# Attention of an encoder in whole f32 instead of split halves, and row sums from blocks added beforehand

## The chip, the cores and the metric

The kernel runs on one core of a Trainium2 chip. Its time is the device time of one execution in microseconds (us); lower is better. Before the change three runs had a median of 2032.31 us (2031.08 to 2033.2). A profiled execution of the same program, from which every duration below is read, took 2032.38 us, of which the trace covers a span of 2030.4 us.

The engines are named as in the profile: PE is the matrix engine (PEld its weight loads), DVE the vector engine, ACT the scalar engine, POOL the GpSimd engine, SP the queue that issues most transfers. PSUM is the memory in which PE leaves its products, in eight banks.

## The reference, cut to what matters

Two layers over 1024 tokens of width 1024, all in float32. One layer:

```python
h = _rmsnorm(x, g_pre_mix[l])
zf, zq, zk, zv, zm = jnp.split(h @ w_in[l], splits, axis=-1)
y_f = _fourier_mix(zf, w_fourier[l])                  # 256 wide
y_a = _window_attn(rope(zq), rope(zk), zv, sink[l])   # 8 query heads, 2 key heads, window of 128 either way
y_m = _memory_attn(zm, km, vm)                        # 4 heads over 256 memory rows
y = concat([_rmsnorm(y_f, gg[:256]), _rmsnorm(y_a, gg[256:768]), _rmsnorm(y_m, gg[768:])]) @ w_out[l]
x = x + _rmsnorm(y, g_post_mix[l])
gate, up = jnp.split(_rmsnorm(x, g_pre_ffn[l]) @ w_ffn_in[l], 2, axis=-1)
x = x + _rmsnorm((jax.nn.silu(gate) * up) @ w_ffn_out[l], g_post_ffn[l])
```

Heads are 64 wide. The three group norms before `w_out` each need the sum of squares of a token's row in their group.

## The kernel before, in words

Large products use a split: an f32 value is rounded to the shorter type `fp32r` (the high part, made on ACT) and the remainder (the low part, made on DVE or POOL) is rounded as well; three products of parts (`Acc.add`, L185) stand for one f32 product. A product of plain f32 operands is also possible; PE does it in two passes, so that the trace has two instructions for each.

A layer goes through these stages. The first layer's times are in brackets, the second layer's lie about 1005 us later.

- Fourier part, keys, values and memory queries (`kvz`, L714, and `kvz_turn`, L731; 60 to 126 us). `kvz_turn` transposes the memory queries on PE and `q_stacks` (L431) puts them into stacks: of two heads that lie on partitions 0 to 63 and 64 to 127, one stack has head 0's high part on the lower 64 partitions and its low part on the upper 64, and the other has head 1's, mirrored. `dup_stacks` (L420) writes a key's high part on both halves, and its low part on both halves. One product over 128 partitions then sums high and low parts of the query against the high part of the key, a second against the low part.
- Queries and memory attention (`q`, L761; `q_turn`, L766; `mem_scores`, L891; `mem_turn`, L917; `mem_values`, L928; 126 to 205 us). A call of `mem_scores` takes one head and 512 tokens: 8 fp32r products 256 wide.
- Attention of key head 0 (`att_units(0)`), woven with the Fourier and memory part of the output product (`fm_units`, L1006; 205 to 292 us). For each block of 128 queries, `att_scores` (L777) makes the scores of four query heads over up to 384 keys, two products a head (L788), DVE adds the mask and takes the maximum, ACT takes the exponential, POOL scales; `att_values` (L817) transposes the weights on PE (L825), splits them (L837) and multiplies (L840); `fold` adds the two halves.
- Attention of key head 1 (`att_units(1)`), woven with the rest of the output product (`out`, L1061), both norms and the transposes for the feed-forward part (`Blocks.tile`, L1099; 292 to 386 us). Here `att_values` takes plain f32 weights and values (L833): the product for the heads of even index writes PSUM partitions 0 to 63, that for the odd ones 64 to 127.
- Feed-forward (L1181, L1330).

`group_scale` (L980) makes the factor of a group norm: ACT squares the group's blocks (2 blocks of 128x128 for the memory group, 4 for the attention group), PE multiplies each block with a 128x2 tile of ones into the same PSUM tile (L988), DVE and POOL make the factor. It runs 16 times per layer.

PSUM tiles come from four pools, `sc`, `pT`, `av` and `pd`, of two tiles each; a tile has one bank. A tile's next user waits until its readers are done.

The order on each engine is set by a scheduler at build time: it places the instructions of all stages by readiness and priority, and each engine then works through its own list in that order. Rings such as `mps` and `yys` give out buffers in turn; a region in `TURNED` changes its type between f32 and fp32r.

## Time and profile before

| | |
|---|---|
| median of three runs | 2032.31 us |
| the profiled execution's own time | 2032.38 us |
| span in the trace | 2030.4 us |
| busy, share of the span | PE 98%, PEld 80%, DVE 74%, ACT 52%, POOL 34% |
| granted TensorE clock, mean | 0.994 of full speed |
| stages that the change touches | about 60 to 390 us and 1060 to 1395 us |

A busy time is the union of an engine's instructions in the trace. PE's ends are modelled and include the time in which a product drains, so the end of one matmul lies after the start of the next, and a short wait of PE can hide under such an end. Distances between starts are therefore used for the price of a matmul. A row of the timeline merges neighbouring instructions of a line: it has the start of the first, the time from there to the end of the last, and their count.

### The profile page before, as it was taken

To read this page: it belongs to the slowest core of one execution; us is meant where nothing else is said; L and a number is where in the kernel's file an instruction comes from. 1 tells how busy PE (TensorE), PEld (TensorE's weight loads), DVE (VectorE), ACT (ScalarE), POOL (GpSimd) and SP (SyncE) were. 2 spreads that over 40 slices of the span, in tenths; PEclk is the share of its full clock that TensorE was granted. 3 is DMA by queue.
4 is the path that set the end of the run, shared out by engine and by line. 5 is a ranking of instruction groups with operands and counts; after the bars stand their busy time and mean duration, and the time that the engine had idled before them with its cause. 6 is when DMAs were issued, how large, how long until landed. Compare 5 with 4: busy or idle time off the path is not lost.

```text
span 2030.4 us, 28325 instructions
## 1 busy us (share of the span) xinstructions
PE 1984.7 (98%) x9587; PEld 1631.2 (80%) x9587; DVE 1492.6 (74%) x2346; ACT 1049.7 (52%) x2204; POOL 684.9 (34%) x811
## 2 busy tenths in 40 slices
PE   8999999999999999999999999999999999999998
PEld 7877878778888888887888778877788888887886
DVE  5566767897877776778876668679786776778766
ACT  6476877643333333554555768686333333346441
POOL 4344445224334333002423644451433433410011
PEclk9999999999999999999999999999999999999999
DMA  6110333434333324879831113244333323269973
GB/s 213 62 58 22 109 104 115 146 109 130 104 109 100 103 88 139 297 266 324 286 142 54 54 58 115 85 144 135 106 118 114 116 82 114 96 209 354 314 265 125
DMA packets 181889, 288.56 MB, mean 142 GB/s; under 512 B 15560, under 2 KB 81648, under 8 KB 181744
## 3 DMA queue, kind: packets, MB, share of 16 engines
q1 hardware_dynamic: 173680, 267.88, 39.7%
q10 hardware_dynamic: 8064, 18.88, 2.4%
q8 instruction: 75, 1.23, 0.2%
q14 instruction: 70, 0.57, 0.1%
HBM read 220.11 MB, written 66.58 MB: 141 GB/s over the span
## 4 chain that ended last, share of the span: by engine, by line
PE 86%; DVE 5%; DMA 3%; ACT 2%; issue 2%; POOL 1%; SPq 0%; DVEq 0%; POOLq 0%; ACTq 0%
PE fo L1330 17%; PE qc L1181 11%; PE qx L1181 11%; PE qy L1181 11%; PE mo L187 8%; PE qz L1181 5%; PE kvp L187 4%; PE qp L187 3%; PE zT L187 2%; PE sc L788 2%; PE pT L825 2%; PE av L833 1%; PE qa L1181 1%; PE mav L932 1%; PE av L840 1%
## 5 line engine op out<-in xcount | busy, mean ns | idle before, releaser
L1330 PE MATMUL fo<-arena_r 128*128 128x512 f32 x1512 | 354.2, 391 | 6.0 <-ACT big L1355 3.8
L1330 PEld LDWEIGHTS fo<-arena_r 128*128 128x128 f32 x1512 | 283.6, 188 | 65.6 <-ACT big L1355 4.6
L176 ACT CAST arena_r<-arena_f 128x512 fp32r<-128x512 f32 (+2 forms) x344 | 185.9, 571 | 179.5 <-DMA arena_f<-actd 66.6
L1181 PE MATMUL qc<-arena_r,flex 128*128 128x512 f32 x912 | 220.2, 390 | 0.0
L177 DVE TENSOR_TENSOR arena_r<-arena_f,arena_r 128x512 fp32r<-128x512 f32 x262 | 182.0, 727 | 46.9 <-ACT arena_r L176 39.0
L1171 ACT CAST flex<-arena_f 128x512 fp32r<-128x512 f32 x148 | 91.9, 621 | 235.0 <-PE qy L1181 73.3
L1181 PEld LDWEIGHTS qc<-arena_r,flex 128*128 128x128 f32 x912 | 171.2, 188 | 37.0
L1181 PE MATMUL qy<-arena_r,flex 128*128 128x512 f32 x576 | 139.9, 390 | 2.3 <-ACT flex L1171 2.3
L1171 ACT CAST arena_r<-arena_f 128x512 fp32r<-128x512 f32 x92 | 57.1, 621 | 159.1 <-DVE arena_f L1168 63.6
L1172 DVE TENSOR_TENSOR flex<-arena_f,flex 128x512 fp32r<-128x512 f32 x148 | 110.9, 750 | 28.4 <-ACT flex L1171 28.2
L1181 PEld LDWEIGHTS qy<-arena_r,flex 128*128 128x128 f32 x576 | 107.9, 188 | 25.3 <-ACT flex L1171 2.7
L1215 POOL TENSOR_TENSOR arena_f<-arena_f 128x512 f32<-128x512 f32 x36 | 47.3, 1315 | 237.5 <-ACT arena_f L1186 237.5
L1181 PE MATMUL qx<-arena_r 128*128 128x512 f32 x360 | 119.5, 389 | 0.0
L1181 PE MATMUL qy<-arena_r 128*128 128x512 f32 x480 | 116.7, 390 | 0.0
L1172 DVE TENSOR_TENSOR arena_r<-arena_f,arena_r 128x512 fp32r<-128x512 f32 x92 | 68.2, 742 | 63.2 <-ACT arena_r L1171 62.8
L1181 PE MATMUL qz<-arena_r,flex 128*128 128x512 f32 x320 | 106.8, 395 | 0.0
L1181 PEld LDWEIGHTS qy<-arena_r 128*128 128x128 f32 x480 | 90.3, 188 | 18.9 <-ACT arena_r L1171 0.2
L1168 DVE TENSOR_TENSOR arena_f<-arena_f 128x512 f32<-128x512 f32 x90 | 98.1, 1098 | 5.5 <-DMA arena_f<-in_w_ffn_in 3.9
L1222 POOL TENSOR_TENSOR arena_f<-arena_f 128x512 f32<-128x512 f32 x36 | 60.0, 1667 | 120.2 <-DVE arena_f L1221 120.2
L187 PE MATMUL mo<-big,arena_r 128*128 128x512 f32 x384 | 100.2, 399 | 0.3 <-ACT arena_f L1031 0.2
L1181 PE MATMUL qx<-flex,flex 128*128 128x512 f32 x304 | 100.1, 390 | 0.0
L1242 POOL TENSOR_TENSOR arena_f<-arena_f,flex 128x512 f32<-128x512 f32 x32 | 51.8, 1619 | 139.5 <-ACT flex L1233 83.7
(315 smaller groups left out, 4659.8 us busy)
## 6 DMA issues: line engine op xcount, KB each, us to landing
arena_f<-in_w_ffn_out SPq DMA_DIRECT2D x264, 256.0 KB, 4.7
actd<-arena_f SPq DMA_DIRECT2D x154, 256.0 KB, 2.5
arena_f<-actd SPq DMA_DIRECT2D x154, 256.0 KB, 4.4
arena_f<-in_w_ffn_in SPq DMA_DIRECT2D x46, 512.0 KB, 3.7
big<-in_w_ffn_in SPq DMA_DIRECT2D x40, 512.0 KB, 4.5
arena_f<-in_w_in SPq DMA_DIRECT2D x40, 256.0 KB, 2.9
arena_f<-in_x SPq DMA_DIRECT2D x16, 512.0 KB, 4.3
arena_f<-in_w_out SPq DMA_DIRECT2D x32, 256.0 KB, 2.7
```

Source lines behind the costliest of these rows:

```text
L176: nc.scalar.copy(hi, src)
L177: return (lo_eng or nc.vector).tensor_tensor(out=lo, in0=src, in1=f32(hi), op=ALU.subtract)
L187: mm(self.dst, a, b, start=self.i == 0, stop=self.i == self.n - 1)
L788: mm(pt, lhs, self.kst[g][i][:, k0 * P : k1 * P], start=i == 0, stop=i == 1)
L1168: nc.vector.tensor_tensor(out=s, in0=x, in1=y, op=op)
L1171: self.cast = nc.scalar.copy(w[:, 0], s)
L1172: nc.vector.tensor_tensor(out=w[:, 1], in0=s, in1=f32(w[:, 0]), op=ALU.subtract)
L1181: mm(pt, a, b, start=start and n == 0, stop=n == 11, skip_group_check=not start)
L1215: G(out=self.u2, in0=self.u2, in1=self.p1, op=ALU.add)
L1222: G(out=self.p5, in0=self.p1, in1=self.p5, op=ALU.add)
L1242: (G if i % 2 else V).tensor_tensor(out=a[i], in0=c, in1=g[i], op=ALU.mult)
L1330: mm(pt, ab[:, 0, x, sl], ab[:, 1, y], start=new and first and j == 0, stop=last and j == 2, skip_group_check=not new)
```

## The change

It does four things.

- **Plain f32 in the window and memory attention.** `q_stacks`, `dup_stacks` and `fold` go. Queries, keys, values and memory queries are copied once, as f32. Two heads of 64 channels stay on partitions 0 to 63 and 64 to 127, and each score is one f32 product over its own 64 partitions: `att_scores` makes two such products, one for each half of the partitions, into the two banks of one tile. `mem_scores` takes two heads and 256 tokens per call instead of one head and 512. `att_values` uses for key head 0 what it had for key head 1; half of its copies for key head 0 go to DVE.
- **A new PSUM pool `s2`** with one tile of two banks for these scores. `qa` of the feed-forward part moves to it, `qc` goes from `pT` to `sc`, `qx` from `sc` to `pT`, `yfp` from `sc` to `av`.
- **Row sums.** `group_scale` adds the squared blocks on DVE (4 to 2 to 1, or 2 to 1) and makes one product with ones. Of 96 products with ones, 32 are left.
- **Storage.** More regions change their type in turn; blocks of the feed-forward part and the ring `yys` move.

```diff
-TURNED = {32: 8, 56: 8, 112: 8, 120: 4}
-PS_BUFS = {"sc": 2, "pT": 2, "av": 2, "pd": 2}
+PS_BUFS = {"sc": 2, "pT": 2, "av": 2, "pd": 2, "s2": 1}
...
-            raw = at(32, 2, NMEM)
-            nc.sync.dma_start(raw, kvd[self.l, :, 0:512].rearrange("p (i c) -> p i c", i=2))
+            self.k = at(32, 2, NMEM)
+            nc.sync.dma_start(self.k, kvd[self.l, :, 0:512].rearrange("p (i c) -> p i c", i=2))
             self.v = at(6, 2, 4, HD)
             nc.sync.dma_start(self.v, kvd[self.l, :, 512:1024].rearrange("p (t h d) -> p t h d", t=2, h=4))
-            km = shaped(reflex(F32R), (2, 2, 2, NMEM))
-            self.km = [km[:, i] for i in range(2)]
-            for ci in range(2):
-                dup_stacks([(self.km[ci][:, j, 0], self.km[ci][:, j, 1]) for j in range(2)], raw[:, ci])
 
...
+            self.kvr = {}
 
         def kvz(self, t):
             half, c = divmod(t, 4)
             if c == 0:
-                self.vst[half] = at(96 + 4 * half, 4, 2, 2, HD, dt=F32R)
-                z = at(104 + 8 * half, 2, 2, 512, dt=F32R)
-                self.zst[half] = [z[:, i] for i in range(2)]
                 if half == 0:
-                    kst = at(80, 2, 2, S, dt=F32R)
-                    self.kst = [[kst[:, i, j] for j in range(2)] for i in range(2)]
+                    self.v32 = turned(96, 2, 2, NT, HD)[:, 0]
+                    self.zf = turned(104, 2, 2, 512)
+                    self.kf = turned(80, 2, S)
             pt = ps([512], "kvp")
             wmov(self.wkvz, self.hT, t, pt)
             r = kvs(512)
             nc.scalar.activation(r, pt, AF.Copy, scale=rx[:, t : t + 1])
-            vst = self.vst[half][:, c]
-            split(vst[:, :, 0, :], vst[:, :, 1, :], r[:, P : 2 * P].rearrange("p (g d) -> p g d", g=2), nc.gpsimd)
+            nc.gpsimd.tensor_copy(self.v32[:, :, t, :], r[:, P : 2 * P].rearrange("p (g d) -> p g d", g=2))
...
-            q_stacks([self.zst[half][j][:, :, c * P : c * P + P] for j in range(2)], zt)
+            nc.scalar.copy(self.zf[:, half, :, c * P : c * P + P], zt)
...
                 ktf = self.kt.rearrange("p c t -> p (c t)")
                 sl = slice(half * 512, half * 512 + 512)
-                dup_stacks([(self.kst[g][0][:, sl], self.kst[g][1][:, sl]) for g in range(2)], ktf)
+                for g, copy in enumerate((nc.scalar.copy, nc.vector.tensor_copy)):
+                    for o in range(2):
+                        copy(self.kf[64 * o : 64 * o + 64, g, sl], ktf[64 * g : 64 * g + 64])
...
-                self.qst[half] = [at((64, 0)[half] + 8 * i, 4, 512, dt=F32R) for i in range(2)]
-            q_stacks([self.qst[half][j][:, :, c * P : c * P + P] for j in range(2)], qt)
+                self.qf[half] = turned((64, 72)[half], 4, 512)
+            nc.scalar.copy(self.qf[half][:, :, c * P : c * P + P], qt)
 
 
...
-            for h in range(4):
-                pt = ps([W], "sc", "sc")
-                lhs = self.qst[half][h % 2][:, 2 * g + h // 2, c * P : c * P + P]
-                for i in range(2):
-                    mm(pt, lhs, self.kst[g][i][:, k0 * P : k1 * P], start=i == 0, stop=i == 1)
-                nc.vector.tensor_tensor_reduce(
-                    out=es_[h // 2][:, h % 2, :W], in0=pt, in1=mask[:, m0 : m0 + W], op0=ALU.add, op1=ALU.max,
-                    scale=1.0, scalar=-3e38, accum_out=rmax[:, h : h + 1],
-                )
+            for hp in range(2):
+                pt = ps([2, 512], "sc", "s2")
+                pts = [pt[:, s, :W] for s in range(2)]
+                for s in range(2):
+                    r = slice(64 * s, 64 * s + 64)
+                    mm(pts[s], self.qf[half][r, 2 * g + hp, c * P : c * P + P], self.kf[r, g, k0 * P : k1 * P], start=True, stop=True)
+                for s in range(2):
+                    nc.vector.tensor_tensor_reduce(
+                        out=es_[hp][:, s, :W], in0=pts[s], in1=mask[:, m0 : m0 + W], op0=ALU.add, op1=ALU.max,
+                        scale=1.0, scalar=-3e38, accum_out=rmax[:, 2 * hp + s : 2 * hp + s + 1],
+                    )
             hs = slice(4 * g, 4 * g + 4)
...
-                if g:
-
-                    pf = self.pfs[self.pfi % 4]
-                    self.pfi += 1
-                    nc.scalar.copy(pf, pT.rearrange("p (k s) q -> p s k q", s=2))
-                    for s in range(2):
-                        rhs = pf[:, s].rearrange("p k q -> p (k q)")
-                        mm(av[64 * s : 64 * s + 64, 0 : 2 * P], self.v32[:, k0 + j], rhs, start=j == 0, stop=j == nk - 1)
-                    continue
-                pp = phs(2, 512, dt=F32R)
-                ph, pl = pp[:, 0], pp[:, 1]
-                split(ph, pl, pT.rearrange("p h q -> p (h q)"))
-                lhs = self.vst[(k0 + j) // 4][:, (k0 + j) % 4, g].rearrange("p a d -> p (a d)")
-                for i, p_ in enumerate((ph, pl)):
-                    mm(av, lhs, p_, start=j == 0 and i == 0, stop=j == nk - 1 and i == 1)
+                pf = self.pfs[self.pfi % 4]
+                self.pfi += 1
+                (nc.vector.tensor_copy if (self.pfi % 2 and not g) else nc.scalar.copy)(pf, pT.rearrange("p (k s) q -> p s k q", s=2))
+                for s in range(2):
+                    rhs = pf[:, s].rearrange("p k q -> p (k q)")
+                    mm(av[64 * s : 64 * s + 64, 0 : 2 * P], self.v32[:, g, k0 + j], rhs, start=j == 0, stop=j == nk - 1)
+            nc.scalar.copy(dst, av[:, 0 : 2 * P].rearrange("p (k q) -> p k q", k=2))
+
+        def att_begin(self, g):
+
+            pf = turned((16, 112)[g], 4, 2, 2, P)
+            self.pfs, self.pfi = [pf[:, i] for i in range(4)], 0
             if g:
...
             nmx = sm(4, "nmx")
             den = sm(4, "den")
-            for b in range(2):
-                pt = ps([2, NMEM], "ms", "sc")
+            pt = ps([2, 2, NMEM], "ms", "s2")
+            pts = [pt[:, s] for s in range(2)]
+            for j in range(2):
+                c = 2 * b + j
+                for s in range(2):
+                    r = slice(64 * s, 64 * s + 64)
+                    mm(pts[s][:, j], self.zf[r, half, pr, c * P : c * P + P], self.mem.k[r, pr], start=True, stop=True)
+            for s in range(2):
+                nc.vector.tensor_reduce(out=nmx[:, 2 * s : 2 * s + 2], in_=pts[s], axis=AX.X, op=ALU.max, negate=True)
                 for j in range(2):
-                    c = 2 * b + j
-                    lhs = self.zst[half][h % 2][:, h // 2, c * P : c * P + P]
-                    for i in range(2):
-                        mm(pt[:, j], lhs, self.mem.km[h // 2][:, h % 2, i], start=i == 0, stop=i == 1)
-                bs = slice(2 * b, 2 * b + 2)
-                nc.vector.tensor_reduce(out=nmx[:, bs], in_=pt, axis=AX.X, op=ALU.max, negate=True)
-                for j in range(2):
-                    c = 2 * b + j
+                    i = 2 * s + j
                     nc.scalar.activation(
-                        e[b][:, j], pt[:, j], AF.Exp, bias=nmx[:, c : c + 1], accum_out=den[:, c : c + 1]
+                        e[s][:, j], pts[s][:, j], AF.Exp, bias=nmx[:, i : i + 1], accum_out=den[:, i : i + 1]
                     )
             rden = sm(4, "rden")
...
-        def mem_values(self, pr, half, pfs):
-            av = ps([512], "mav", "av")
+        def mem_values(self, half, pr, b, pfs):
+            av = ps([256], "mav", "av")
             for mt in range(2):
                 for s in range(2):
-                    mm(av[64 * s : 64 * s + 64], self.mem.v[:, mt, 2 * pr + s], pfs[s][mt], start=mt == 0, stop=mt == 1)
-            nc.vector.tensor_copy(self.ym[half][:, pr, :], av)
+                    mm(av[64 * s : 64 * s + 64], self.mem.v[:, mt, 2 * pr + s], pfs[mt][:, s], start=mt == 0, stop=mt == 1)
+            nc.vector.tensor_copy(self.ym[half][:, pr, 256 * b : 256 * b + 256], av)
 
         def mem_units(self):
-            todo = [(h, half) for half in range(2) for h in range(4)]
+            todo = [(half, pr, b) for half in range(2) for pr in range(2) for b in range(2)]
...
+            while w > 1:
+                w //= 2
+                nc.vector.tensor_tensor(out=sq[:, :w], in0=sq[:, :w], in1=sq[:, w : 2 * w], op=ALU.add)
             pss = ps([2], "ssp", "av")
-            for i in range(w):
-                mm(pss, sq[:, i], ones, start=i == 0, stop=i == w - 1)
+            mm(pss, sq[:, 0], ones, start=True, stop=True)
             ms = sm(1, "ms")
             nc.vector.tensor_scalar(out=ms, in0=pss[:, 0:1], scalar1=1.0 / n, scalar2=EPS, op0=ALU.mult, op1=ALU.add)
...
-        HB = {1: (64, 72), 2: (80, 88), 5: (16, 24), 6: (96, None), 3: (0, 8), 7: (32, 40), 4: (104, None)}
+        HB = {1: (64, 104), 2: (80, 72), 5: (16, 24), 6: (96, None), 3: (0, 8), 7: (32, 40), 4: (88, None)}
...
-            pt = ps([512], "qa", "sc")
+            pt = ps([512], "qa", "s2")
...
-                self.c11 = ps([512], "qc", "pT")
+                self.c11 = ps([512], "qc", "sc")
...
-                self.x = ps([512], "qx", "sc")
+                self.x = ps([512], "qx", "pT")
...
+        mix.att_begin(0)
...
+            if i == 5:
+                reflex(F32R, 64)
+                reflex(F32R, 104)
...
+                for k in (72, 80, 112):
+                    reflex(F32R, k)
                 gq.step(1)
```

The scheduler makes a new order of it. Three places of the lists follow, each as it stands before and after the change. The names are those of the tiles: `sc` are window scores, `mav` the memory values, `ssp` the row sum, `mo` the output product, `pT` transposes of the weights, `hTp` transposes for the feed-forward part, `qc` its first product. A row has line, operation, output and inputs, the size, and how many follow one another; an f32 product is one row's count here, though it is two instructions in the trace.

PE, in the first layer, where the attention of key head 0 begins, before:

```order
L788 MATMUL sc_2269<-arena_r 128x384 x2
L932 MATMUL mav_2085<-arena_f 64x512 x3
L788 MATMUL sc_2273<-arena_r 128x384 x2
L988 MATMUL ssp_2148<-const,arena_f 128x2 x2
L788 MATMUL sc_2277<-arena_r 128x384 x2
L988 MATMUL ssp_2234<-const,arena_f 128x2 x2
L187 MATMUL mo_2126<-big_2038,arena_r 128x512 x3
L187 MATMUL mo_2126<-big_2039,arena_r 128x512 x3
L788 MATMUL sc_2281<-arena_r 128x384 x2
```

and after:

```order
L763 MATMUL sc_2193<-flex_841,flex_1484 128x384 x2
L887 MATMUL mav_2020<-flex_110,arena_f 64x256 x2
L944 MATMUL ssp_2085<-const,arena_f 128x2
L763 MATMUL sc_2198<-flex_841,flex_1484 128x384 x2
L187 MATMUL mo_2062<-big_1970,arena_r 128x512 x3
L187 MATMUL mo_2062<-big_1971,arena_r 128x512 x3
L944 MATMUL ssp_2165<-const,arena_f 128x2
L187 MATMUL mo_2070<-big_1968,arena_r 128x512 x3
```

Where four heads had four score tiles in turn, two heads now share one tile, and the block's second pair (`sc_2198`) stands behind one pair of memory values and one row sum.

DVE at the same place, before:

```order
L789 ISA arena_f,rmax_2268<-sc_2269,const 128x384
L789 ISA rmax_2268 128x1
L795 SCALAR_TENSOR_TENSOR nmx_2175<-rmax_2158,const 128x4
L805 TENSOR_TENSOR es_2185<-nmx_2175,const 128x4
L933 COPY arena_f<-mav_2085 128x512
L789 ISA arena_f,rmax_2268<-sc_2273,const 128x384
```

and after:

```order
L765 ISA arena_f,rmax_2192<-sc_2193,const 128x384
L765 ISA rmax_2192 128x1
L765 ISA arena_f,rmax_2192<-sc_2193,const 128x384
L765 ISA rmax_2192 128x1
L783 TENSOR_TENSOR den_2107<-den_2107,es_2115 128x4
L888 COPY arena_f<-mav_2020 128x256
L942 TENSOR_TENSOR arena_f<-arena_f 128x128
L946 TENSOR_SCALAR ms_2087<-ssp_2085 128x1
L785 RECIPROCAL rden_2119<-den_2107 128x4
L989 TENSOR_TENSOR arena_f<-mo_2053,arena_f 128x512
L942 TENSOR_TENSOR arena_f<-arena_f 128x128
L765 ISA arena_f,rmax_2192<-sc_2198,const 128x384
```

The readers of a pair now stand together, and an add of squared blocks (L942), which waits for ACT's square, stands ahead of the readers of the next pair.

PE at the end of the first layer's attention, before:

```order
L1106 MATMUL hTp_4051<-const,arena_f 128x128 x4
L1106 MATMUL hTp_4059<-const,arena_f 128x128 x4
L988 MATMUL ssp_3931<-const,arena_f 128x2 x2
L187 MATMUL mo_4007<-flex_90,arena_r 128x512 x3
L187 MATMUL mo_4007<-arena_r 128x512 x6
L187 MATMUL mo_4007<-flex_91,arena_r 128x512 x3
L187 MATMUL mo_4021<-flex_90,arena_r 128x512 x3
L187 MATMUL mo_4021<-arena_r 128x512 x6
L187 MATMUL mo_4021<-flex_91,arena_r 128x512 x3
L1181 MATMUL qc_4071<-arena_r,flex_4070 128x512 x12
```

and after:

```order
L807 MATMUL av_3696<-flex_2851,arena_f 64x256 x4
L1137 MATMUL qc_3861<-flex_3436,flex_3860 128x512
L1137 MATMUL qc_3861<-flex_3437,flex_3860 128x512
L1137 MATMUL qc_3899<-flex_3436,flex_3860 128x512
L1137 MATMUL qc_3899<-flex_3437,flex_3860 128x512
L1062 MATMUL hTp_3839<-const,arena_f 128x128 x4
L1137 MATMUL qc_3861<-flex_3436,flex_3860 128x512 x2
```

The first feed-forward products, which stood behind the last output products, now stand ahead of them: two `qc` tiles are begun before the last `mo` tiles.

77 lines of the change are left out of this document (22 added, 55 removed).

## The prediction

> **What bounds the kernel now.** I read the page's first and fourth part, then the busy time by stage, then PE's groups by form, then single rows of the timeline.
>
> ```profile
> span 2030.4 us, 28325 instructions
> PE 1984.7 (98%) x9587; PEld 1631.2 (80%) x9587; DVE 1492.6 (74%) x2346; ACT 1049.7 (52%) x2204; POOL 684.9 (34%) x811
> PE 86%; DVE 5%; DMA 3%; ACT 2%; issue 2%; POOL 1%; SPq 0%; DVEq 0%; POOLq 0%; ACTq 0%
> ```
>
> PE holds 86% of the chain that ended last. The view by stage (length; then busy time and count of PE, PEld, DVE, ACT, POOL; clock; DMA share; GB/s) says the same of the stages that are changed; the sum is over three stretches of the first layer and the three of the second that answer to them.
>
> ```profile
> 126.00:205.00 79.00, 76.90 (x399) 59.82 (x397) 50.72 (x83) 50.70 (x137) 39.01 (x64) 0.98 0.12 38
> 205.00:292.00 87.00, 84.52 (x453) 70.31 (x452) 65.32 (x199) 68.29 (x182) 38.83 (x65) 1.00 0.34 114
> 292.00:386.00 94.00, 91.65 (x530) 72.05 (x530) 66.92 (x133) 66.97 (x166) 45.76 (x78) 0.98 0.39 131
> sum 520.00, PE 508.19 PEld 404.39 DVE 370.72 ACT 375.31 POOL 248.67; mean PE 84.70 PEld 67.40 DVE 61.79 ACT 62.55 POOL 41.44
> ```
>
> PE is idle for 11.8 us of 520; DVE and ACT have a good quarter free. Work taken off DVE or ACT therefore counts only through PE's waits; work added to or taken off PE counts in full. So the sum is one of PE's prices, and then of its waits.
>
> **Row sums.** PE's groups (out<-in, rows*columns, size, count | busy, mean ns | idle before):
>
> ```profile
> L988 PE MATMUL ssp<-const,arena_f 128*128 128x2 f32 x192 | 26.2, 240 | 1.1 <-DVE arena_r L438 1.1
> L788 PE MATMUL sc<-arena_r 128*128 128x384 f32 x192 | 49.0, 355 | 0.1
> L901 PE MATMUL ms<-flex,arena_r 128*128 128x256 f32 x64 | 10.4, 289 | 2.1 <-ACT flex L425 1.3 <-DVE flex L438 0.8
> L833 PE MATMUL av<-flex,arena_f 128*64 128x256 f32 x176 | 26.3, 398 | 0.0
> L932 PE MATMUL mav<-arena_f 128*64 128x512 f32 x64 | 23.4, 612 | 0.0
> L840 PE MATMUL av<-arena_r 128*128 128x512 f32 x88 | 31.0, 420 | 2.2 <-DVE flex L863 2.0 <-DVE arena_r L177 0.2
> L1106 PE MATMUL hTp<-const,arena_f 128*128 128x128 f32 x128 | 19.5, 283 | 1.8 <-DVE arena_f L321 1.8
> L1181 PE MATMUL qa<-arena_r,flex 128*128 128x512 f32 x48 | 12.9, 404 | 2.5 <-ACT flex L1171 2.5
> ```
>
> The 192 rows of L988 are 96 products in two passes each. Mean and busy time contain the drain, so the price comes from starts:
>
> ```profile
> 212.35 0.59 PE L788 MATMUL sc<-arena_r 128*128 128x384 f32 x2
> 212.78 0.50 PE L988 MATMUL ssp<-const,arena_f 128*128 128x2 f32 x4
> 213.14 1.64 PE L187 MATMUL mo<-big,arena_r 128*128 128x512 f32 x6
> ```
>
> From 212.78 to 213.14 two row-sum products take 0.36 us, 0.18 each. 64 of 96 go: -11.5 us; by the mean distance in longer rows, about 0.11 a pass, it is -14. I take **-13**.
>
> DVE gets 48 adds of 128 x 128 or 256 elements (16 for the memory group, 32 for the attention group). The nearest row is an add of 256 elements:
>
> ```profile
> L578 DVE TENSOR_TENSOR arena_f<-arena_f 128x256 f32<-128x256 f32 x16 | 6.5, 464 | 0.0
> L177 DVE TENSOR_TENSOR arena_r<-pT,arena_r 128x512 fp32r<-128x512 f32 x44 | 29.4, 687 | 1.3 <-ACT arena_r L176 0.8
> L438 DVE TENSOR_TENSOR arena_r<-qT,arena_r 64x512 fp32r<-64x512 f32 x32 | 22.0, 689 | 9.9 <-ACT arena_r L435 9.4
> L863 DVE TENSOR_TENSOR flex<-av,flex 64x256 f32<-64x256 f32 x32 | 13.2, 413 | 1.0 <-ACT flex L861 0.7
> ```
>
> At 0.46 for 256 and some 0.3 for 128 that is 17 us of DVE time, with 22 copies of transposed weights at about 0.69 (15 us). The other three rows, 64.6 us, go. DVE comes out about 30 us lighter in these stages, so the adds lie in freed time. If DVE bound here, they would cost their 17 us.
>
> **Window scores.** Before, a head is two products. From 212.35 to 212.78 they take 0.43; four in one row take 0.35 a head:
>
> ```profile
> 306.94 0.87 PE L788 MATMUL sc<-arena_r 128*128 128x384 f32 x4
> 307.64 0.50 PE L988 MATMUL ssp<-const,arena_f 128*128 128x2 f32 x4
> 308.07 1.52 PE L833 MATMUL av<-flex,arena_f 128*64 128x256 f32 x12
> 309.52 0.72 PE L187 MATMUL mo<-flex,arena_r 128*128 128x512 f32 x2
> ```
>
> With 96 heads 384 wide at about 0.41 and 32 heads 256 wide at 0.33, that is 50 us now. The new product on half of the rows is nowhere in the trace; the nearest thing is a product on half of the columns:
>
> ```profile
> 168.22 0.65 PE L932 MATMUL mav<-arena_f 128*64 128x512 f32 x2
> 198.50 1.94 PE L932 MATMUL mav<-arena_f 128*64 128x512 f32 x8
> 200.37 1.09 PE L922 MATMUL mpT<-const,arena_f 128*128 128x128 f32 x8
> 299.73 0.62 PE L788 MATMUL sc<-arena_r 128*128 128x384 f32 x2
> 300.28 0.65 PE L833 MATMUL av<-flex,arena_f 128*64 128x256 f32 x4
> 300.86 0.44 PE L825 MATMUL pT<-const,arena_f 128*128 128x128 f32 x2
> ```
>
> In the first row, a look at 0.1 us of the timeline, two matmuls of L932's 0.61 on average fit into 0.65: they start together, so two halves of the columns run at once. A pair of products (four passes) 256 wide takes 0.58 to the next start. Three pairs take 1.45 (308.07 to 309.52), so a further pair is 0.43 and the group's own charge 0.15. Two pairs 512 wide take 1.87, so 0.86 a pair. Before the group, 299.73 to 300.28 is 0.55 for what takes 0.43 elsewhere: another 0.1 to change over. For halves of the rows I take the same, and 0.05 more since a load is 128 columns instead of 64:
>
> ```profile
> L988 PEld LDWEIGHTS ssp<-const,arena_f 128*128 128x128 f32 x192 | 27.5, 193 | 8.5 <-issue 4.2 <-PE mpT L922 1.0 <-DVE arena_r L438 0.5
> L833 PEld LDWEIGHTS av<-flex,arena_f 128*64 128x64 f32 x176 | 9.7, 135 | 8.0 <-issue 4.4 <-ACT arena_f L316 0.5 <-ACT arena_f L801 0.5
> ```
>
> A pair 384 wide is then 0.65 + 0.30 = 0.95, one 256 wide 0.73. 48 and 16 pairs make 57 us; the order tears four pairs apart, which costs each of them a second time, 3.4 us. 61 against 50: **+11**. Bounds: +4 without the wider load and the torn pairs; if the halves of the rows do not run at once, 48 x 0.65 + 16 x 0.43 = 38 us more.
>
> The Trainium skill, in TensorEngine Tiling (Array Packing), section Key Properties, says that a change of tiling mode drains the engine while tiles of one mode run in parallel. The trace agrees for columns (0.10 + 0.15 a group, two at once); nothing here shows rows. Without that drain, about 0.25 for each of the 80 new row groups, the whole sum would come out 20 us lower.
>
> **Memory scores and values.** A row of the chain of waits has eight of the old score products:
>
> ```profile
> 176.11 0.95 PE ms L901 x8
> ```
>
> 128 at 0.12 are 15 us, some 17 with their starts. New: 16 calls of two pairs, 0.73 + 0.43 = 1.16, with four calls torn: about 20. **+3.** The values keep their passes, with twice as many, shorter products in whole pairs more often than before: **-1**, between -4 and +2.
>
> **Values of key head 0.** 88 products at 0.23 (four start to start like L187's, 213.14) are 20 us. The new form is L833's, whose 88 products cost 26 us and their change-overs: **+6**, between +3 and +8.
>
> PE's own work is thus -13 + 11 + 3 - 1 + 6 = +6 us.
>
> **Waits.** Three of the idle times above lose their cause: L840 waits for the split and the fold (2.2), L901 for the stacked memory keys (2.1), L988 for a stack of the queries (1.1). The waits at the end of the attention (hTp 1.8, qa 2.5) find `qc` products ahead of them in the new order; I count half, 2. What shows as idle is only what exceeds a drain of some 0.17 us, so I add as much again, 5 or 6, for the hidden part: **-13**. What is late next is the score tile: the second pair of a block now waits until DVE has read the first.
>
> ```profile
> L789 DVE CUSTOM_DVE_ANT_0 arena_f<-sc,const 128x384 f32<-128x384 f32 x96 | 51.2, 552 | 24.6 <-PE sc L788 14.7 <-PE pT L825 5.6 <-POOL arena_r L177 3.0
> L789 DVE DVE_READ_ACCUMULATOR2_ANT rmax<- 128x1 f32 x128 | 10.6, 83 | 0.0
> ```
>
> Two reads are 2 x 0.63 = 1.3 us. Behind the waiting product stands everything else of PE. The order puts 2 to 7 us of other products between most pairs, but under 1 us between the first two or three pairs of each layer: **+2**.
>
> The sum is +6 - 13 + 2 = -5 us on the profiled execution's 2032.38 (span 2030.4 and 2 us around it), which is the median of 2032.31 within 0.1. Forecast: **2027 us**.
>
> **Rivals.**
> - *The waits give more.* DVE's and ACT's relief takes away the small waits that hide under the drains in all six stretches, and row pairs cost no wider load: -15 further, **2012**. For it: 370 us of DVE work shrinks. Against: PE is 98% busy already.
> - *The single score tile binds* (slower). If half of the 64 pairs wait 0.7 us for their two reads, because DVE has an add that waits for ACT's square, or a weight split, ahead of them, that is 22 us: **2047**. It decides from the point where less than 1.5 us of other work lies between two pairs. The Trainium skill, in TensorEngine Tiling (Array Packing), section PSUM Bottleneck, says that tiling speeds up the products but not the reading of PSUM; PE's idle before L788 was only 0.1 us with two tiles.
> - *Row halves run one after the other* (slower): 38 us for the window scores and 32 x 0.43 = 14 for the memory scores, **2079**. No row speaks to it but the column halves, which do run together.
> - *Change-overs are dearer than priced*, by 0.15 for each of the 80 row groups: +12, **2039**.
>
> **How the numbers follow.** Forecast 0.45 (its own range 2018 to 2036), more from the waits 0.22, score tile 0.15, rows in turn 0.09, dearer change-overs 0.09. About 0.2%, 4 us, is what a measurement here tells from no change. Faster: 0.26 of the forecast's own, and 0.22 = 0.48. Same: 0.16 + 0.03 = 0.19. Slower: 0.03 + 0.15 + 0.09 + 0.06 = 0.33. Range 2010 to 2050: it leaves out rows in turn (0.09), some of the score-tile case above (0.05) and of the second case below (0.06).
>
> **What would show it.** Starts of a score pair within 0.1 us of each other, and some 0.95 from one pair to the next product, confirm the price; about 1.6 means rows in turn. The row sums should show 64 matmul rows. PE's wait for `rmax` or L765 above 10 us means that the score tile binds. Idle before `mav`, `ms` and `av` should vanish. I am wrong if PE's work between 126 and 386 us shrinks or grows by more than 10 us, or if the time changes outside the attention stages.

## The result and the profile after

The change made the kernel slower: 2067.93 us (2066.7 to 2070.7, four runs) against 2031.69 (2030.53 to 2033.2, four runs) before. The ratio is 1.0182, 95% interval 1.0166 to 1.0197. The forecast was 2027 us, the range ended at 2050. The profiled execution of the changed kernel, the slowest of the four, has a span of 2068.9 us, 38.5 more than before.

The first and fourth part of its page, which answer to the first three lines that the prediction shows:

```profile
span 2068.9 us, 28051 instructions
PE 2006.1 (97%) x9611; PEld 1585.9 (77%) x9611; DVE 1431.3 (69%) x2260; ACT 1000.8 (48%) x2094; POOL 701.1 (34%) x809
PE 78%; DVE 7%; DMA 5%; issue 3%; ACT 3%; POOL 3%; DVEq 0%; SPq 0%; POOLq 0%; ACTq 0%
```

DVE and ACT did become lighter, by 61 and 49 us. PE became busier by 21, and its share of the chain that ended last fell from 86 to 78%: the chain now runs through DVE, transfers, ACT and POOL more often. PE's busy time alone therefore does not say where 38 us come from. The lengths of the stages do. Below are five of eleven stretches, cut where a stage's first product starts (length; then busy time and count of PE, PEld, DVE, ACT, POOL; clock; DMA share; GB/s). Before the change:

```profile
0.00:67.00 67.00, 53.82 (x327) 48.92 (x328) 36.65 (x70) 43.34 (x86) 29.73 (x54) 0.95 0.56 183
204.00:404.00 200.00, 195.17 (x1075) 158.21 (x1075) 148.54 (x355) 145.88 (x367) 86.92 (x146) 0.99 0.36 120
808.00:1039.00 231.00, 226.54 (x1064) 189.01 (x1063) 179.26 (x267) 117.03 (x217) 45.74 (x46) 1.00 0.83 283
1122.00:1202.00 80.00, 77.95 (x413) 60.52 (x413) 53.37 (x90) 54.60 (x146) 41.84 (x70) 1.00 0.15 46
1202.00:1403.00 201.00, 197.37 (x1087) 157.90 (x1086) 150.72 (x356) 149.30 (x373) 89.81 (x146) 1.00 0.35 119
```

and with the change:

```profile
0.00:71.00 71.00, 53.93 (x324) 48.46 (x325) 36.60 (x70) 43.73 (x86) 30.18 (x54) 0.88 0.54 172
208.00:421.00 213.00, 203.53 (x1054) 135.16 (x1050) 139.04 (x344) 135.62 (x345) 90.19 (x145) 0.98 0.33 111
825.00:1062.00 237.00, 229.31 (x1069) 190.72 (x1068) 181.78 (x269) 117.72 (x219) 46.10 (x48) 0.99 0.81 277
1148.00:1234.00 86.00, 81.40 (x442) 58.97 (x442) 38.48 (x64) 45.97 (x125) 42.72 (x72) 0.98 0.17 50
1234.00:1441.00 207.00, 201.25 (x1063) 136.02 (x1060) 140.65 (x343) 136.34 (x344) 84.92 (x143) 1.00 0.33 111
```

In order: the start, up to the first keys (+4 us), the attention of the first layer (+13), its feed-forward output (+6), and in the second layer the memory attention (+6) and the attention (+6). The six stretches left out give the other 3.5. So about a quarter of the loss, 10.5 us, lies in the start and the feed-forward part, where the prediction looked for nothing.

To separate price from waiting I went through the starts of PE's instructions. For each kind of matmul (shape, place in its group, kind of the neighbour before and behind) the lower quartile of the distance to the next start, over both traces, is its price; what exceeds it is wait. By this reckoning PE's price went from 1940 to 1952 us (**+12.6**) and its waits from 76.6 to 102.7 us (**+26.1**). With the quartile taken over the traces of all runs instead of these two, it is +9 and +29, so the split is good to some 3 us. The prediction had +6 and -11. The price is the smaller part of the miss, the waits are the larger. They lie in the first layer's attention (about +9), in the second layer's keys and memory attention (+8), in the two feed-forward outputs (+8 together) and in the start (+4); the second layer's attention has +2.

Not all of what exceeds the price is waiting. The mean granted clock was 0.994 before and 0.990 in this execution, so 12 and 21 us of clock were not granted: up to 9 of the 26 us are products that ran slower (last section).

### The profile page after: what moved, and what is told of

Its sections match the earlier page's. It is cut to its first block, busy times and chain, and to the rows that moved or that the text cites. A ratio compares the mean times of both kernels' runs of the same rounds, so it can differ in the third digit from the quotient of the medians.

```text
span 2068.9 us, 28051 instructions
## 1 busy us (share of the span) xinstructions
PE 2006.1 (97%) x9611; PEld 1585.9 (77%) x9611; DVE 1431.3 (69%) x2260; ACT 1000.8 (48%) x2094; POOL 701.1 (34%) x809
## 4 chain that ended last, share of the span: by engine, by line
PE 78%; DVE 7%; DMA 5%; issue 3%; ACT 3%; POOL 3%; DVEq 0%; SPq 0%; POOLq 0%; ACTq 0%
PE fo L1286 15%; PE qy L1137 10%; PE qx L1137 10%; PE qc L1137 10%; PE mo L187 7%; PE qz L1137 5%; PE qp L187 4%; PE kvp L187 4%; PE sc L763 2%; PE zT L187 2%; PE pT L801 2%; PE av L807 2%; DMA arena_f<-actd 1%; DMA arena_f<-in_w_ffn_out 1%; DVE flex L177 1%
## 5 line engine op out<-in xcount | busy, mean ns | idle before, releaser
L1286 PE MATMUL fo<-flex 128*128 128x512 f32 x1176 | 283.1, 394 | 6.6 <-ACT big L1311 3.7
L1286 PEld LDWEIGHTS fo<-flex 128*128 128x128 f32 x1176 | 222.2, 190 | 53.7 <-ACT big L1311 4.1
L1137 PE MATMUL qc<-flex,flex 128*128 128x512 f32 x912 | 221.2, 391 | 2.2 <-ACT flex L1127 1.8
L176 ACT CAST flex<-arena_f 128x512 fp32r<-128x512 f32 (+1 forms) x228 | 130.1, 606 | 156.4 <-DMA arena_f<-actd 72.5
L1137 PEld LDWEIGHTS qc<-flex,flex 128*128 128x128 f32 x912 | 170.8, 188 | 40.0 <-ACT flex L1127 2.9
L177 DVE TENSOR_TENSOR flex<-arena_f,flex 128x512 fp32r<-128x512 f32 x204 | 146.0, 741 | 65.0 <-ACT flex L176 53.8
L1286 PE MATMUL fo<-arena_r 128*128 128x512 f32 x672 | 165.5, 393 | 4.3 <-ACT big L1311 4.3
L1286 PEld LDWEIGHTS fo<-arena_r 128*128 128x128 f32 x672 | 126.7, 189 | 31.0 <-ACT big L1311 4.7
L1128 DVE TENSOR_TENSOR flex<-arena_f,flex 128x512 fp32r<-128x512 f32 x148 | 109.9, 744 | 28.4 <-ACT flex L1127 28.2
L1137 PE MATMUL qx<-flex,arena_r 128*128 128x512 f32 x384 | 125.8, 390 | 0.0
L1128 DVE TENSOR_TENSOR arena_r<-arena_f,arena_r 128x512 fp32r<-128x512 f32 x92 | 68.1, 741 | 63.9 <-ACT arena_r L1127 63.7
```

Of the source, the lines that this page charges most:

```text
L176: nc.scalar.copy(hi, src)
L177: return (lo_eng or nc.vector).tensor_tensor(out=lo, in0=src, in1=f32(hi), op=ALU.subtract)
L1128: nc.vector.tensor_tensor(out=w[:, 1], in0=s, in1=f32(w[:, 0]), op=ALU.subtract)
L1137: mm(pt, a, b, start=start and n == 0, stop=n == 11, skip_group_check=not start)
L1286: mm(pt, ab[:, 0, x, sl], ab[:, 1, y], start=new and first and j == 0, stop=last and j == 2, skip_group_check=not new)
```

## What a tiled group costs its neighbours

PE's groups after the change (out<-in, rows*columns, size, count | busy, mean ns | idle before):

```profile
L944 PE MATMUL ssp<-const,arena_f 128*128 128x2 f32 x64 | 10.2, 228 | 0.0
L763 PE MATMUL sc<-flex,flex 64*128 64x384 f32 x192 | 48.0, 550 | 0.8 <-DVE rmax L765 0.8
L763 PE MATMUL sc<-flex,flex 64*128 64x256 f32 x64 | 12.0, 431 | 0.1
L857 PE MATMUL ms<-arena_f,flex 64*128 64x256 f32 x128 | 19.1, 405 | 1.7 <-ACT arena_f L862 1.7
L187 PE MATMUL mo<-flex,arena_r 128*128 128x512 f32 x192 | 57.4, 406 | 2.2 <-DVE arena_f L1028 2.0
L187 PE MATMUL mo<-arena_r 128*128 128x512 f32 x192 | 55.7, 401 | 1.3 <-POOL arena_r L177 1.3
L887 PE MATMUL mav<-arena_f 128*64 128x256 f32 x96 | 18.5, 424 | 2.7 <-ACT arena_f L879 2.7
L801 PE MATMUL pT<-const,arena_f 128*128 128x128 f32 x352 | 59.6, 282 | 1.7 <-POOL arena_f L788 1.2 <-DVE flex L804 0.3
```

The row sums have their 64 matmul rows, the window scores are 60 us (the prediction: 61). But the 352 transposes of the weights, which the change does not touch, went from 53.4 to 59.6 us of busy time. By starts (distances to the next start, waits included) they went from 33.4 to 44.5, all transposes together by 25. Single rows of the timeline show why; each piece has four transposes `pT` and what stands ahead of and behind them:

```profile
274.36 1.64 PE L187 MATMUL mo<-big,arena_r 128*128 128x512 f32 x6
275.83 0.60 PE L801 MATMUL pT<-const,arena_f 128*128 128x128 f32 x4
276.19 0.71 PE L187 MATMUL mo<-big,arena_r 128*128 128x512 f32 x2
...
279.19 0.66 PE L801 MATMUL pT<-const,arena_f 128*128 128x128 f32 x4
279.60 0.47 PE L187 MATMUL mo<-big,arena_r 128*128 128x512 f32 x1
...
313.16 0.60 PE L801 MATMUL pT<-const,arena_f 128*128 128x128 f32 x4
313.69 0.59 PE L763 MATMUL sc<-flex,flex 64*128 64x384 f32 x2
...
315.99 0.39 PE L807 MATMUL av<-flex,arena_f 128*64 128x256 f32 x2
316.30 0.66 PE L801 MATMUL pT<-const,arena_f 128*128 128x128 f32 x4
316.89 0.92 PE L763 MATMUL sc<-flex,flex 64*128 64x384 f32 x4
317.74 0.66 PE L801 MATMUL pT<-const,arena_f 128*128 128x128 f32 x4
```

Between two products of the whole array (275.83 to 276.19) four transposes take 0.36 us. Behind a tiled group they take 0.41 (279.19, behind `av`, to 279.60), ahead of one 0.53 (313.16), between two 0.59 (316.30). The four values repeat within 0.01 us wherever no wait falls in. So transposes are 0.17 us longer where a tiled group follows them, and 0.06 longer where they follow one. An fp32r product is 0.09 longer where a tiled group follows it.

Of the 0.17, 0.08 is not the tiling's. In both kernels an fp32r product behind transposes starts early by the record, and then takes 0.31 to the next start instead of 0.23. Ahead of a plain f32 product of the whole array the four transposes take 0.43, as in the run on whole rows below:

```profile
259.09 0.60 PE L802 MATMUL pT<-const,arena_f 128*128 128x128 f32 x4
259.52 0.82 PE L762 MATMUL sc<-flex,flex 128*128 128x192 f32 x4
```

Measured from there, entry is 0.10 behind transposes, about the same as behind an fp32r product. And the group pays in its own rows as well. A lone pair of scores takes 0.85 to the next start (316.89 to 317.74), but two pairs that stand in one group, in the run with two tiles below, take 1.49:

```profile
211.61 1.56 PE L762 MATMUL sc<-flex,flex 64*128 64x384 f32 x8
213.10 0.65 PE L885 MATMUL mav<-arena_f 128*64 128x256 f32 x4
```

The second pair is 0.64, so 0.2 is the group's own charge, close to the 0.15 + 0.05 that the prediction took. What it did not count is what the rows beside a group pay. In price, transposes, output products and query products became 21 us dearer (part of it the 0.08 a time, which before the change stood in the rows of the fp32r scores), row sums became 12.5 cheaper, and scores, memory and values together 4 dearer. Before the change the order had 50 tiled groups, now it has 184.

The Trainium skill, in TensorEngine Tiling (Array Packing), section Key Properties, says that a change of tiling mode drains the engine. The rows agree, and give it a size here: 0.09 to 0.10 us going in and 0.06 on the transposes behind, in the neighbours' rows, and 0.2 in the group's own.

## The experiments

All ratios are against runs of the kernel before on the same chip, whose median lay between 2031.7 and 2033.8 us. I write A for "PE pays for changes of tiling mode", other letters as they come.

**Whole rows.** The scores' two products run over all 128 rows, on half of the columns each.

```diff
-                    mm(pts[s], self.qf[half][r, ...], self.kf[r, g, k0 * P : k1 * P], ...)
+                    mm(pt[:, s, : W // 2], self.qf[half][:, ...], self.kf[:, g, k0 * P + s * W // 2 : ...], ...)
```

> The changed kernel with window scores over all 128 rows and half of the columns each: two products, one after the other, of 192 or 128 columns where two products of 384 or 256 columns ran side by side on half of the rows. The readers on DVE read the half twice, so their time and the tile are the same; the scores themselves are not those of the reference. PE streams the same columns, but the window scores need no change of tiling mode. Theory A: each of some 68 groups loses about 0.09 to 0.17 us before it and 0.06 to 0.1 behind it, 12 to 18 us together, so 2048 to 2056 us. Theory C (the single tile of two banks makes PE wait): the tile is still single, so 2064 us or more.

2051.1 us, ratio 1.0089 (1.0068 to 1.0109), 17 us faster than the changed kernel. PE's groups:

```profile
L762 PE MATMUL sc<-flex,flex 128*128 128x192 f32 x192 | 40.2, 331 | 3.8 <-DVE rmax L766 3.6 <-DVE rden L786 0.2
L762 PE MATMUL sc<-flex,flex 128*128 128x128 f32 x64 | 11.0, 296 | 0.8 <-DVE rmax L766 0.7
```

51 us of busy time instead of 60 for the same streamed columns, and the weights' transposes fell by 6 us in price. The named wait for `rmax` even grew, from 0.8 to 4.3, and the kernel is faster all the same. The order has 109 tiled groups instead of 184. A holds, at about the size that the prediction had named for the drain (20 us), and 17 us is more than the 8 to 11 that a new order alone made (below); C, the single tile, does not hold.

**Two tiles for the scores.** That was tried directly as well.

```diff
-PS_BUFS = {..., "s2": 1}
+PS_BUFS = {..., "s2": 4}
...
-                pt = ps([2, 512], "sc", "s2")
-                pts = [pt[:, s, :W] for s in range(2)]
+                pts = [ps([512], "sc", "s2")[:, :W] for s in range(2)]
```

(and the same for the memory scores).

> The changed kernel with the window and memory scores in two tiles of one bank each instead of one tile of two banks, so that a pair can begin while the pair before is still read, and in any two of the eight banks. The same products and readers. Theory C (the single tile costs, and binds also where the trace names no wait for it): 6 us or more faster than the changed kernel, 2052 to 2062 us, with PE's waits before the scores and in the memory stage of the second layer (9.8 us, before the change 4.7) down to those of before. Theory A with the adds and the ring, but no cost of the tile: 2064 to 2072 us.

2076.8 us, 1.0210 (1.0193 to 1.0228): 9 us slower than the changed kernel by the medians, 6 by the ratios, where C expected it to be faster. PE's groups show no wait before the scores:

```profile
L762 PE MATMUL sc<-flex,flex 64*128 64x384 f32 x192 | 60.3, 525 | 0.0
L762 PE MATMUL sc<-flex,flex 64*128 64x256 f32 x64 | 13.5, 417 | 0.0
```

But they take 74 us. With two tiles a head's product is ready on its own, and the scheduler tore pairs apart: 40 products of a single head stand alone, against 8 with the one tile. A lone product takes 0.84 to the next start where a pair takes 0.85. The memory stage of the second layer did lose 4 us of waits. So this run does not price the single tile by itself: with one tile the pairs stay together, at 60 us of busy time instead of 74, and that outweighs what waits it makes.

**The adds.** Undone in the changed kernel:

```diff
-            while w > 1:
-                w //= 2
-                nc.vector.tensor_tensor(out=sq[:, :w], in0=sq[:, :w], in1=sq[:, w : 2 * w], op=ALU.add)
-            mm(pss, sq[:, 0], ones, start=True, stop=True)
+            for i in range(w):
+                mm(pss, sq[:, i], ones, start=i == 0, stop=i == w - 1)
```

> The change without its adds: every squared block is multiplied with ones again, all else as changed. In the trace of the changed kernel a row-sum product costs 0.12 us and there are 64 products fewer than before, 14 us of PE's starts. Theory A (PE pays for changes of tiling mode, the adds are a gain): 12 to 14 us slower than the changed kernel, about 2080 us. Theory B (the adds stand ahead of the score readers on DVE and hold up the single score tile): faster than the changed kernel, 2045 to 2060 us.

2082.2 us, 1.0241 (1.0215 to 1.0266), the number of A: with their adds the row sums are a gain here, and the rest of the change alone is 50 us slower than before. By stages the 14 us are less clean. PE's price rose by 18 us, its waits in the attention fell by 12, and the other 8 us are waits in the feed-forward output, which has no row sum. The adds alone on the kernel before:

> The kernel before with the adds alone. Theory A: PE loses 64 products of 0.12 to 0.18 us and nothing else, 2018 to 2022 us, against 2032 before. Theory B: DVE's adds cost what PE saves or more, 2032 us or above.

2036.0 us, 1.0028 (1.0012 to 1.0044). Here A is not right. PE's price fell by 16 us, as reckoned, but its waits in the two attention stages grew from 12.2 and 10.4 us to 24.1 and 21.9. (This execution was the slowest of its nine, at 2042.7 us, and its clock was 0.97 and 0.98 in these stages against 0.99 and 1.00 before, so a few us of the growth are slower products.) B, that DVE's time is what costs, was then tried by the same adds on POOL (`nc.gpsimd` for `nc.vector`):

> The kernel before with the adds of squared blocks alone, on POOL instead of DVE. The adds alone on DVE took 2036 us, with 16 us less of PE's own work and 26 us more of its waits. Theory B (on a DVE that is 74% busy the adds hold up PE's other partners): with POOL, 34% busy, most of the waits go, 2018 to 2028 us, faster than before. Theory D (any new order has waits of this kind): 2032 to 2040 us.

2039.7 us, 1.0030 (1.0016 to 1.0043). The waits stay: 25.5 and 20.2 us. PE's waits in the first layer's attention, waiter <- awaited: us, times, longest; first with the adds on DVE, then on POOL:

```profile
PE mo L187 <- DVE arena_f L1074: 3.5, 2, 2.9
```

```profile
PE ssp L990 <- POOL arena_f L988: 7.3, 3, 5.1
PE mo L187 <- DVE arena_f L1074: 3.3, 3, 1.5
```

DVE's load alone does not explain the waits, since they stay without it. What both runs share is the longer chain: square on ACT, one or two adds, product, factor, and only then can L1074 read the output product (`mo`) and give its bank back; PE stands before the row sum or before the next `mo`. Before the change the adding was PE's own, in its own stream. That it is the chain is argued from this order of work and not shown apart: an add on POOL took 0.64 or 0.86 us against 0.40 or 0.54 on DVE, so the second run also made the chain longer. In the changed kernel the adds' rows are

```profile
L942 DVE TENSOR_TENSOR arena_f<-arena_f 128x128 f32<-128x128 f32 x32 | 10.9, 341 | 2.1 <-ACT arena_f L939 2.0
L942 DVE TENSOR_TENSOR arena_f<-arena_f 128x256 f32<-128x256 f32 x16 | 8.0, 499 | 7.6 <-ACT arena_f L939 7.6
```

18.9 us of DVE, close to the 17 reckoned, and 9.7 us in which DVE, which works through its list in order, stands before an add, nearly all of it for ACT's square. What the adds cost there was measured by leaving them out and keeping the one product:

> The changed kernel in which the adds are left out and the one product with ones is kept, so the row sums hold one block instead of two or four: PE's work is that of the changed kernel, DVE has 48 instructions and some 17 us less in each of the two layers together. Theory A: within 4 us of the changed kernel, 2064 to 2072 us. Theory B: 10 us or more faster, below 2058 us.

2060.6 us, 1.0142 (1.0127 to 1.0158), 7 us faster: between the two expectations. PE's waits in the attention fell from 20.7 and 12.3 us to 11.8 and 11.3; some 3 us of the first fall are a clock of 1.00 instead of 0.98. So in the changed kernel the adds give 12.5 us of price and cost 7 to 10 us of waits.

Half of the adds on the kernel before, as a way to a faster version: the first add of the attention group alone, and the add of the memory group alone.

```diff
+            if w == 4:          # the other run: if w == 2: w = 1, with sq[:, :1] and sq[:, 1:2]
+                w = 2
+                nc.vector.tensor_tensor(out=sq[:, :2], in0=sq[:, :2], in1=sq[:, 2:4], op=ALU.add)
```

> The kernel before with the first add of the attention group alone (four blocks to two, then two products; the memory group as it was). The products that go save about 4 us of PE. With all adds, PE's own work fell by 16 us, but its waits in the two attention stages grew by 11 us in each layer, whether the adds were on DVE or on POOL. Theory H (the waits come from the longer chain square, add, add, product, factor, which ends in the output products' readers): half the chain, so 2 to 5 us more of waits in each layer and 2032 to 2040 us. Theory I (it is the last add that costs): 2026 to 2030 us, faster than before.

> The kernel before with the add of the memory group alone (two blocks to one, one product instead of two; the attention group as it was): 16 products of 0.12 to 0.18 us less, 2 to 3 us. The factor is needed one block of queries later, so there is time for the add. Theory H: the chain of the memory group is off the path, 2028 to 2031 us. Theory D (any new order costs, as the two null edits did): 2033 to 2042 us.

2034.4 us, 1.0007 (0.9996 to 1.0019), and 2040.1 us, 1.0035 (1.0017 to 1.0052). The first is no different from before: 8 us of price less, 9 us of waits more. The second misses what H expected, since the price fell by 3 us and the waits rose by 10, though this chain has a block of queries' time to spare; D, below, is left for it. No version here is faster than the kernel before.

**The order alone.** Loads of weights are written one unit earlier, nothing else; the scheduler then makes another order of the same instructions.

```diff
-        weave(mix.mem_units(), q[1:8] + [mix.fm_load] + q[8:])
+        weave(mix.mem_units(), q[1:7] + [mix.fm_load] + q[7:])
```

> The kernel before, with every instruction as it was; only the loads of four blocks of output weights (fm_load) are written one unit of memory attention earlier, so that the scheduler makes another order. Theory D (the order before was a lucky one, and any new order has 15 to 30 us more of waits on PE): 2042 to 2060 us. Theory E (the waits that appeared with the change come from what it does): within 6 us of before, 2026 to 2038 us.

> The kernel before, with every instruction as it was; only the loads of the query weights (q_load) are written one unit earlier. Theory D: 2042 to 2060 us. Theory E: 2026 to 2038 us.

> The changed kernel with the same edit as the first of these runs (fm_load one unit earlier). Theory D: the spread of orders applies here too, anywhere from 2050 to 2078 us. Theory E: within 6 us of the changed kernel, 2062 to 2074 us.

> The changed kernel with the same edit as the second of these runs (q_load one unit earlier). Theory D: anywhere from 2050 to 2078 us. Theory E: 2062 to 2074 us.

The kernel before: 2042.0 us, 1.0055 (1.0034 to 1.0076), and 2041.1, 1.0038 (1.0025 to 1.0052). The changed kernel: 2066.7, 1.0171 (1.0154 to 1.0188), and 2066.7, 1.0170 (1.0154 to 1.0185). For the changed kernel E's range holds; for the kernel before neither theory is right as it stood. Its new orders lose 8 to 11 us, at or below the lower edge of what D expected and beyond what E allowed; their profiled executions lose only 3 and 5 us, since executions of one kernel lie up to 14 us apart here. So a new order can cost 0.4 to 0.55% by itself, and the differences of 0.17 to 0.35% among the edits of the kernel before cannot be put to the edits alone. Most of the loss is none of that: from the worse order of before (1.0055) to the better one of the changed kernel (1.0170) there is still 1.1%.

**The ring of the feed-forward output.** Its first stall in the changed kernel, in the chain of waits between 818 and 860 us (start, length, what):

```profile
819.29 2.81 PE qz L1137 x12
...
822.64 0.69 DVE arena_r L177
...
823.35 6.30 DMA arena_f<-actd
...
857.93 0.50 ACT big L1311
...
858.47 1.87 PE fo L1286 x5
```

The chain does not stay on PE. It leaves the last product of the feed-forward input (`qz`, of block 4), goes to the split into a second buffer at 822.64, to a load that could only start then, and through more splits and loads to ACT's copies of `fo` at 857. The change moved block 4 from place 104 to 88. In the first layer 88 is the second buffer in the ring of the feed-forward output (`abs_`), and 104 is the last. Undone, and done to the kernel before:

```diff
-        abs_.ks = (64, 72, 80, 88, ..., 56, 104, 112) if last else (80, 88, 96, 48, 56, 104)
+        abs_.ks = (64, 72, 80, 104, ..., 56, 88, 112) if last else (80, 104, 96, 48, 56, 88)
```

> The changed kernel with two places of the ring of buffers in the feed-forward output exchanged (88 and 104). With the change, block 4 of the feed-forward input lies at 88, the ring's second place in the first layer and fourth in the second; its product is the last of the feed-forward input, so the second buffer may come free only at its end. Before, block 4 lay at 104, the last place but one or the last. Up to the feed-forward output the order is that of the changed kernel. Theory F (this holds up the first loads of the feed-forward output, whose two stages take 236.5 + 216.0 us with the change and 231.2 + 213.8 before): 6 to 9 us faster than the changed kernel, 2058 to 2062 us. Theory G (these stages are longer by chance of transfers): 2064 to 2070 us.

> The kernel before with the same two places of the ring exchanged, so that block 4 (here at 104) now takes the second place, as it does with the change. Theory F: 5 to 9 us slower than before, 2037 to 2041 us, in the feed-forward output alone. Theory G: 2030 to 2034 us.

The changed kernel: 2065.1 us, 1.0152 (1.0130 to 1.0174), 3 us faster by the medians and 6 by the ratios. In this run the order up to the feed-forward output is the same, so it can be read stage by stage: the first layer's output took 232.1 us instead of 236.5, the second's 215.7 instead of 216.0. The same place in the chain:

```profile
820.61 2.80 PE qz L1137 x12
823.41 2.75 PE qx L1137 x12
826.16 29.25 PE fo L1286 x129
...
857.06 0.50 ACT big L1311
...
857.60 2.58 PE fo L1286 x10
```

PE now holds the chain without a break for 35 us. The kernel before with the exchange: 2038.95 us, 1.0030 (1.0016 to 1.0044), where PE's wait for ACT's copies of `fo` went from 0.9 to 3.5 us in the first layer and from 2.9 to 5.3 in the second. F holds for the first layer, at 4 to 5 us. For the kernel before its range is met as well; for the changed kernel as a whole the gain is half of what F expected by the medians.

**Key head 0 alone.** The kernel before with the change's f32 value products for key head 0.

```diff
-                split(ph, pl, pT.rearrange("p h q -> p (h q)"))
-                for i, p_ in enumerate((ph, pl)):
-                    mm(av, lhs, p_, ...)
+                (nc.vector.tensor_copy if (self.pfi % 2 and not g) else nc.scalar.copy)(pf, ...)
+                for s in range(2):
+                    mm(av[64 * s : 64 * s + 64, 0 : 2 * P], lhs, rhs, ...)
```

> The kernel before with the change's value products for key head 0 alone (f32 on column halves, as for key head 1; the values there are the rounded high parts, the small remainder is left out). Column groups grow from 50 to 84. By the prediction: PE's own work +6 us, the wait of L840 gone, 2 to 4 us, so 2034 to 2038 us. Theory A (changes of tiling mode are paid by the neighbours too: 0.09 us before a group behind an fp32r product and 0.17 behind a transpose, 0.06 on a transpose behind it): 34 groups more at 0.15 to 0.2 come to 5 to 7 us on top, 2040 to 2046 us.

2038.6 us, 1.0017 (1.0005 to 1.0028), 3.5 us by the ratio. PE's price rose by 9 to 10 us and its waits fell by 2 to 4. The time fits the prediction's term. The price lies between that term (+6) and what A makes of it (11 to 13), and the difference is inside the uncertainty of an order, so this run does not decide between them.

**Three causes at once.** Whole rows, no adds, and the exchanged ring in the changed kernel.

> The changed kernel with three things taken away at once: window scores over whole rows and half of the columns (as in the run on whole rows), the adds left out with one product kept (so the row sums hold one block), and the two places of the ring exchanged. Apart they gave -17, -7 and -3 us against the changed kernel's 2068. If they are three separate costs the sum is 2039 to 2043 us, 0.4 to 0.6% above before; of the 14 us of PE that the row sums save, the rest of the change then eats all and 8 us more. If they are one and the same slack, freed by whichever goes first, 2049 to 2052 us.

2040.0 us, 1.0048 (1.0029 to 1.0067). The three costs add up: 17 + 7 + 3 from 2068 is 2041. What is left, 10 us above before in spite of 12.5 us of price saved by the row sums, no run explains fully. Of it, key head 0 has 3 to 4. The start (1 to 5 us more of waits) and the keys and memory stage of the second layer (4 to 8 us more of waits, in every version of the changed kernel) stay open: their order and storage changed together, and they were not tried apart. The order itself, at 8 to 11 us, could be much of it.

## Why the prediction was wrong

- *What bounds.* PE at 98% busy, with PE's prices counted in full: right.
- *Row sums, -13:* right. By starts they went from 22.2 to 8.0 us, in price by -12.5.
- *DVE gets 17 us of adds that lie in freed time:* the 17 us were right (18.9), the freed time did not help. **This step failed.** It asked whether the engine has time, and not who waits at the end of the chain that the adds lengthen. The waits that come with the adds cost 7 to 10 us here, and as much as the whole saving on the kernel before. That they come through the chain is the likeliest reading, not a shown one.
- *Window scores, +11:* the mechanism and the size were right. The halves of the rows run side by side: two matmuls of 0.55 us fit into 0.59 at 313.69, and a whole wide pair takes 0.85 to the next start (316.89 to 317.74), with 0.09 ahead of it behind an fp32r product, against 0.95 reckoned. By starts of their own rows the scores grew by 8.0 us, and whole rows gave back 17 us, since the rows beside the groups gain as well.
- *Change-overs:* mis-sized. The prediction took 0.10 going in from one place, behind an fp32r product, and that is right behind transposes too. It left out what a group costs behind it (0.06 on transposes), and it counted 80 row groups, while all tiled groups went from 50 to 184. Memory scores (+0.3 by starts for +3), memory values (+0.8 for -1) and key head 0 (+2.8 for +6) came out about as reckoned or better in their own rows; with the rows beside them PE's price is +12.6 instead of +6. The rival of dearer change-overs (+12) was half right.
- *Waits, -13:* **the term that failed**, by 37 us with the +2 for the tile (up to 9 of them slower clock). Of the three named waits two went as foretold (L988 1.1 to 0.0, L840 2.2 to 0.0), and L901's only shrank from 2.1 to 1.7. New ones came, before `mav` (2.7), `mo` (3.5 in two groups), `pT` (1.7), and in the feed-forward output. A trace of before lists the waits that a change can remove; it cannot list those of the new order. The experiments account for 7 to 10 us of them (the adds) and 3 to 6 (storage); the start and the second layer's keys and memory stay open. The doubling of the visible waits for a hidden part, 5 or 6 us, rested on no row.
- *The single tile, +2:* right in size as far as the trace names it, 0.8 us of waits for `rmax`, and the rival of 2047 with it at its core finds no support: two tiles brought no gain.
- *Storage* was told as part of the change and not priced at all. It cost some 3 to 6 us, in a stage that the prediction's last sentence named as a sign of being wrong.

## What to carry to other kernels

A tiled group is paid for in its own first and last products and by its neighbours: count the groups that the order will make, and read the distances ahead of one and behind one, before trading whole-array products for smaller tiles. Work moved off the bounding engine is free only if nothing on that engine waits at the end of the chain it joins; look at who reads the result, not at how idle the new engine is. And when a change moves storage, go through each ring that uses the moved places and ask which buffer comes free last.

## What was not expected of the hardware

The granted clock of PE halves for a few us several times in each kernel, and the length of a stall does not tell when. In the changed kernel PE was idle for 3.7 us up to 858.47 (the wait for L1311 above). Three stretches of 2 us behind it:

```profile
858.00:860.00 2.00, 1.53 (x5) 1.29 (x6) 1.97 (x4) 2.00 (x5) 0.00 (x0) 0.81 0.87 303
860.00:862.00 2.00, 2.00 (x6) 1.52 (x6) 1.46 (x3) 2.00 (x5) 0.00 (x0) 0.50 0.92 287
862.00:864.00 2.00, 2.00 (x9) 1.62 (x8) 1.39 (x2) 0.37 (x1) 0.00 (x0) 0.84 0.98 364
```

Here (1 - 0.81 + 1 - 0.50 + 1 - 0.84) x 2 = 1.7 us of clock were not granted, so it was 0.50 for 3.4 us. In the kernel before, at the same place, the wait was 0.9 us and the clock stayed at 1.00. The Trainium skill, in TensorE: Matmul & The Clock Gate, section What's actually happening, puts the limit at an idle window of about 3.4 us; 3.7 and 0.9 lie on the two sides of it. But other stretches do not fit, if that window is to be idle throughout. In the kernel before PE was idle for only 1.8 us up to 373.53 (the wait of `hTp` for L321), and the clock fell all the same:

```profile
372.00:374.00 2.00, 0.47 (x5) 0.50 (x6) 1.90 (x3) 1.23 (x4) 1.57 (x3) 1.00 0.43 172
374.00:376.00 2.00, 2.00 (x11) 2.00 (x10) 2.00 (x4) 0.92 (x2) 0.00 (x0) 0.50 0.65 185
```

And an idle stretch of 2.2 us, up to 412.9 in the changed kernel, was followed by no fall: the clock stayed at 1.00 to 418. What decides is not shown here.

The other surprise is the scheduler's: two orders of the same instructions, apart by where a few loads are written, differ by 0.4 to 0.55%, more than most single edits tried here.
